# Delta rule on one Trainium2 core: the 16-to-32 step of the triangular inverse, from DVE products to matmuls

## The chip, the cores and the metric

The kernel runs on one core of one Trainium2 chip. The metric is the device time of one execution in microseconds; three timed runs of the kernel before gave 1537.31, 1538.44 and 1539.12, with a median of 1538.44 us.

## The reference

One decoder layer over 1024 tokens of width 1024, in float32. The normalised input is projected once; its columns feed four gated DeltaNet heads (head size 128) and eight forgetting-attention heads. Both outputs go through an output projection, a SwiGLU feed-forward block, a gated input embedding and a last norm. What the change touches is the triangular solve inside the chunked delta rule, cut here to its core:

```python
gc = jnp.cumsum(g, axis=-1)                    # per chunk of 64 tokens
kk = jnp.einsum('bnhid,bnhjd->bnhij', kb, k) * decay
a_mat = jnp.where(strict, kk, 0.0) + jnp.eye(CHUNK)
rhs = jnp.concatenate([vb, kb * jnp.exp(gc)[..., None]], axis=-1)
sol = lax.linalg.triangular_solve(a_mat, rhs, left_side=True, lower=True, unit_diagonal=True)
u, w = sol[..., :dv], sol[..., dv:]
...
v_new = u_c - jnp.einsum('bhcd,bhde->bhce', w_c, state)    # then a scan over the chunks
```

## The kernel before

All of the layer runs on one core, in stages: norm and value projection, then the stage of the change (from about 80 to 480 us of the span), then attention and output projection, then the feed-forward block and the rest.

In the stage of the change TensorE (PE) is fed from one order that is written out while the program is built. `weave` (line 221) holds a list of generators (the streams of the delta rule) and one filler, `projections` (line 670), whose `project` issues 24 matmuls `pj` of 512 columns for each half of a projected block. When a stream says it is ready, its matmuls are issued next; otherwise the filler gives one group of three. "Ready" is decided by `Plan` (lines 53 to 129), which keeps a clock of its own: a DVE operation on n elements is priced at 0.06 + n/960 us, an ACT operation at 0.09 + n/1200, a handoff from one engine to another at 0.377, one behind another on the same engine at 0.13, a DMA at 0.7 + bytes/360e3 + 1, and an f32 matmul of 128 columns at 4 x 128/2400. The order on PE is thus fixed: a matmul whose operand comes later than the plan thought stops PE, with the filler behind it.

The delta rule works in units of 128 tokens, eight for each head, handled as two groups g of four (tiles of 128 x 4 x 128). For each head h the streams are:

- `prep` (704): transposes, norms and gates; it makes nT (the negated strictly triangular matrix, transposed) and stores it to DRAM (n_d).
- `base` (765): all 32 blocks of 32 rows of the head's eight units, one partition for each (four copies over the 128 partitions), are read back as nb. DVE inverts 8-row blocks by seven steps, joins pairs to 16 rows (two products for each of the two 16-row blocks), and joins those to 32 rows (copies to uq, then four products: x times nb, then that times ub). A product is one `tensor_tensor` of 512 elements and one `tensor_reduce`. The blocks go to DRAM (u_d) by one DMA for the lower 16-row block and four for uq. `fence` makes later DVE work wait behind each of the three bursts.
- `inv` (824), twice for each head: loads U from u_d, transposes it on DVE in 32 x 32 blocks into T, then PE makes px = nT by T, ACT copies it, PE makes pz, and DVE writes pz into U where `mask` says so: the step from 32 to 64. A similar step on half the partitions goes from 64 to 128, and pw and pu follow.
- `scan` (901): the recurrence over eight units, whose pr, pS and po matmuls each wait for a small DVE operation (vT or Ss).

`prep_heads` and `inv_heads` order the heads: `prep` of head h+1 starts when `base` of head h is planned, `base` of head h+1 when `inv` of head h and `prep` of head h+1 are. Outside PE a scheduler orders each engine by the program; DVE, ACT and the SP queue, which issues nearly all DMAs, run in order. `gates` (513) makes ngc, the negated cumulative gate, which `prep` reads as a bias.

Of the kernel before, what the change touches and what calls it, by code (L numbers as in the profile page):

```python
# [8 lines left out]
F32 = mybir.dt.float32  # L9
# [3 lines left out]
I8 = mybir.dt.int8  # L13
AF = mybir.ActivationFunctionType
ALU = mybir.AluOpType
# [4 lines left out]
P = 128  # L20
S = 1024
DM = 1024
NT = S // P
KT = DM // P
HALF = 512
GH = 4
# [161 lines left out]
def hybrid_layer(ctx, tc, x, p, attn_norm_w, w_in, conv_w, a_log, dt_bias, gdn_norm_w, fox_f_bias,  # L188
# [3 lines left out]
    V, A, G, PE, SY = (Engine(tc, e, n) for e, n in zip((nc.vector, nc.scalar, nc.gpsimd, nc.tensor, nc.sync), "VAGPD"))  # L192
# [17 lines left out]
    def mm(ps, lhsT, rhs, start=True, stop=True, more=False):  # L210
        PE.matmul(ps, lhsT=lhsT, rhs=rhs, start=start, stop=stop, **(dict(skip_group_check=True) if more else {}))
# [31 lines left out]
    def ready(*ins, slots=(), extra=0.0):  # L243
        return poll(lambda: wait(*ins, slots=slots), extra)
# [21 lines left out]
    const = Pool(tc, name="const", bufs=1, side="left")  # L266
# [41 lines left out]
    B2 = HS // 4  # L308

    def dview(tl, offset, dims):  # L310
        a = tl[:]
        return bass.AP(tensor=a.tensor, offset=a.offset + offset, ap=dims)
# [77 lines left out]
    def gpt(name, tag="a"):  # L390
        return dict(a=psa, s=pss, o=pso)[tag].tile([P, 4, P], F32, tag=tag, name=name)
# [75 lines left out]
    mask = const.tile([P, P], I8, name="mask")  # L467
    V.scalar_tensor_tensor(mask, xm, 64.0, ge, op0=ALU.is_lt, op1=ALU.mult)

    xin.close()  # L470

    def load_w(c, name):
# [17 lines left out]
    def g4(tag, name, bufs=1, dt=F32, pool=None):  # L490
        pool = pool or (gpb if tag in ("scr", "nT", "X") else gp)
        return pool.tile([P, 4, P], dt, tag=tag, name=f"{tag}_{name}", bufs=bufs)
# [14 lines left out]
    egl = const.tile([P, NT, GH], F32, name="egl")  # L507
    egt = const.tile([P, NT, GH], F32, name="egt")
    kdw = const.tile([P, NT, GH], F32, name="kdw")
    ngc = const.tile([P, NT, GH], F32, name="ngc")  # L510
    beta = const.tile([P, NT, GH], F32, name="beta")

    def gates():
        def flat(tl):
            return tl.rearrange("p a b -> p (a b)")

        s0, s1, s2 = (flat(g4("scr", f"gates{i}", 4)) for i in range(3))
        zg, eg, ug, lgu = (s0[:, P * i:P * i + P].rearrange("p (t c) -> p t c", c=16) for i in range(4))
        ru = s1[:, 0:P].rearrange("p (t c) -> p t c", c=16)
        lf = s1[:, P:P + 64].rearrange("p (t c) -> p t c", c=FH)  # L520
        V.tensor_tensor(zg[:, :, 0:12], gat[:, :, 0:12], gb.unsqueeze(1).to_broadcast([P, NT, 12]), op=ALU.add)
        V.tensor_copy(zg[:, :, 12:16], gat[:, :, 12:16])
        V.tensor_scalar(zg[:, :, 0:8], zg[:, :, 0:8], -1.0, None, op0=ALU.mult)
        V.scalar_tensor_tensor(eg, zg, -1.0, zg, op0=ALU.mult, op1=ALU.min)
        A.activation(eg, eg, AF.Exp)
        V.tensor_scalar(ug, eg, 1.0, None, op0=ALU.add)
        A.activation(lgu, ug, AF.Ln)
        V.reciprocal(ru, ug)
        V.scalar_tensor_tensor(ug, ug, -1.0, eg, op0=ALU.add, op1=ALU.subtract)
        V.tensor_tensor(ug, ug, ru, op=ALU.mult)  # L530
        V.tensor_tensor(lgu, lgu, ug, op=ALU.subtract)
        V.scalar_tensor_tensor(lgu, zg, 0.0, lgu, op0=ALU.max, op1=ALU.add)
        V.scalar_tensor_tensor(beta, zg[:, :, 12:16], 0.0, eg[:, :, 12:16], op0=ALU.is_ge, op1=ALU.max)
        V.tensor_tensor(beta, beta, ru[:, :, 12:16], op=ALU.mult)
        V.tensor_scalar(lf, lgu[:, :, 0:8], -1.0, None, op0=ALU.mult)
        A.activation(alog, alog, AF.Exp)
        V.scalar_tensor_tensor(gg, lgu[:, :, 8:12], -1.0, alog.unsqueeze(1).to_broadcast([P, NT, GH]),
                               op0=ALU.mult, op1=ALU.mult)
        zz = gpa.tile([P, S], F32, tag="vt", name="zz", bufs=2)
        G.memset(zz, 0.0)  # L540
        yield from ready(gg)
        ggf, gcf, eglf, kdwf = (a.rearrange("p t h -> p (t h)") for a in (gg, gc, egl, kdw))
        gl = flat(gpt("gl"))
        mm(gl[:, 0:32], tri, ggf)
        mm(gl[:, 32:64], ones, ggf)
        V.tensor_copy(gcf, gl[:, 0:32])
        V.tensor_scalar(ngc.rearrange("p t h -> p (t h)"), gl[:, 0:32], -1.0, None, op0=ALU.mult)
        V.tensor_tensor(kdwf, gl[:, 32:64], gcf, op=ALU.subtract)
        A.activation(eglf, gl[:, 32:64], AF.Exp)
        A.activation(kdwf, kdwf, AF.Exp)  # L550
        A.activation(egt.rearrange("p t h -> p (t h)"), gcf, AF.Exp)
        crow = gpa.tile([P, S], F32, tag="vt", name="crow", bufs=2)[0:FH]
        G.memset(s2[0:FH], 1.0)
        for hf in range(2):
            ps = flat(gpt(f"lfT{hf}"))
            for j in range(4):
                tr(ps[0:FH, j * P:(j + 1) * P], lf[:, hf * 4 + j, :], ident)
            V.tensor_tensor_scan(crow[:, hf * HALF:(hf + 1) * HALF], s2[0:FH], ps[0:FH, :],
                                 0.0 if hf == 0 else crow[:, HALF - 1:HALF], op0=ALU.mult, op1=ALU.add)
        yield from ready(gc, slots=[SA])  # L560
        ps = flat(gpt("gcT"))
        tr(ps[0:32, 0:P], gcf, ident)
        gcs = s1[0:32, 2 * P:3 * P]
        A.activation(gcs, ps[0:32, 0:P], AF.Copy)
        SY.dma_start(gc_d, gcs)
        for img_ in u_d:
            SY.dma_start(img_.rearrange("(p a c) -> p a c", a=2, c=HS // 32),
                         zz[:, 0:HS // 32].unsqueeze(1).to_broadcast([P, 2, HS // 32]))
        cs_ = []
        for i in range(2):  # L570
            q = gpa.tile([P, 2, S], F32R, tag="kq", name=f"crs{i}", bufs=2)
            cs_ += [q[0:FH, 0], q[0:FH, 1]]
        split(cs_[0], cs_[1], crow)
        V.tensor_scalar(cs_[2], f(cs_[0]), -1.0, None, op0=ALU.mult)
        V.tensor_scalar(cs_[3], f(cs_[1]), -1.0, None, op0=ALU.mult)
        for a in range(4):
            SY.dma_start(crow_d[:, a, a // 2, :], f(cs_[a]))
            SY.dma_start(crow_d[:, a, 1 - a // 2, :].rearrange("h (b c) -> h b c", c=P),
                         ones[0:FH].unsqueeze(1).to_broadcast([FH, NT, P]))
        flags["gates"] = True  # L580
# [123 lines left out]
    def prep(h, g):  # L704
        kq, vT = kqv[h]
        nm = f"{h}_{g}"
        t0 = 4 * g
# [30 lines left out]
        V.tensor_tensor(dt_, egb, mbias.unsqueeze(1).to_broadcast([P, 4, P]), op=ALU.add)  # L738
        A.activation(egb, egb, AF.Exp)
        for j in range(4):  # L740
            A.activation(dt_[:, j, :], dt_[:, j, :], AF.Exp, bias=ngc[:, t0 + j, h:h + 1])
        yield from ready(sm, dt_, slots=[SA])
        nT = nTs[h, g] = g4("nT", nm, 4)
        qkT = qkTs[h, g] = g4("qkT", nm, 2 * home(h)[1], pool=home(h)[0])
# [20 lines left out]
    def base(h):  # L765
# [8 lines left out]
        pf = blk("pr")  # L774
        uf = blk("uq")
        u8 = uf[:, 192:448].rearrange("p (b r c) -> p b r c", b=4, c=8)
        uq = uf[:, 0:192].rearrange("p (m i n) -> p m i n", i=3, n=16)
        G.memset(ub, 0.0)
        G.memset(u8, 0.0)
        G.memset(u8.rearrange("p b r c -> p b (r c)")[:, :, 0:64:9], 1.0)  # L780
# [1 line left out]
        def sub(o, n):  # L782
            return nbt[:, o:o + 32 * n].rearrange("p (r c) -> p r c", c=32)[:, :, 0:n]

        def product(out, x, y):
            m, n = x.shape[1], x.shape[2]
            pr = pf[:, 0:m * n * n].rearrange("p (m n k) -> p m n k", n=n, k=n)
            V.tensor_tensor(pr, x.unsqueeze(2).to_broadcast([P, m, n, n]),
                            y.rearrange("p k n -> p n k").unsqueeze(1).to_broadcast([P, m, n, n]), op=ALU.mult)
            return V.tensor_reduce(out, pr, axis=AX.X, op=ALU.add)  # L790

        def fence(last, tile_):
            plan.fence = (last.ins.name, plan.done[plan.key(tile_)][0])
# [15 lines left out]
            last = product(ub[:, b, 0:8, 8:16], w, u8[:, 2 * b + 1])  # L809
        fence(last, ub)  # L810
        yield from ready(ub)
        for q in range(4):
            ps_ = slice(32 * q, 32 * q + 32)
            V.tensor_copy(uq[ps_, :, 0], ub[ps_, 0, 4 * q:4 * q + 4, :])
        for i, o, rhs in ((0, 2, sub(16, 16)), (2, 1, ub[:, 1])):
            for m in (0, 2):
                last = product(uq[:, m:m + 2, o], uq[:, m:m + 2, i], rhs)
        fence(last, uf)
        SY.dma_start(dview(u_d[h], B2 // 2, [[B2, 32], [P, 16], [1, 16]]), ub[0:32, 1])
        for q in range(4):  # L820
            SY.dma_start(dview(u_d[h], 4 * q * P, [[B2, 32], [P, 4], [1, 32]]),
                         uq[32 * q:32 * q + 32, :, 0:2].rearrange("p m i n -> p m (i n)"))

    def inv(h, g):
        nm = f"{h}_{g}"
# [7 lines left out]
        T = g4("X", f"T{nm}", 4)  # L833
        V.transpose(T.rearrange("p a b -> p (a b)"), U.rearrange("p a b -> p (a b)"))
        yield from ready(T, nT, slots=[SA])
        px = gpt(f"px5_{nm}")
        for j in range(4):
            mm(px[:, j, :], nT[:, j, :], T[:, j, :])
        X = g4("X", f"X{nm}", 4)
        A.activation(X, px, AF.Copy)  # L840
        yield from ready(X, slots=[SA])
        pz = gpt(f"pz5_{nm}")
# [926 lines left out]
```

## Time and profile before

| | |
|---|---|
| timed runs, median (lowest, highest) | 1538.44 us (1537.31, 1539.12) |
| the profiled execution's own time | 1536.84 us |
| its span, first to last instruction | 1535.1 us |
| PE busy, share of the span | 1444.3 us, 94% |
| DVE busy | 942.4 us, 61% |
| ACT busy | 628.5 us, 41% |
| mean granted TensorE clock | 0.98 |

The profiled execution is 1.6 us below the median. Matmuls overlap, so a PE that counts as busy need not be at its peak; where PE's queue stands still, the views give the wait and what ended it. The granted clock is in shares of 2.4 GHz; 0.50 is the level of 1.2 GHz.

### The profile page before, as it was taken

Reading aid. Unit: us, or ns where it says so; the run is one execution under the profiler, and the core shown is the slowest. Engines: PE = TensorE matmul, PEld = TensorE weight load, DVE = VectorE, ACT = ScalarE, POOL = GpSimd, SP = SyncE. Lnnn points to the kernel's source line nnn. Section 1 sums busy time; section 2 is a strip of 40 time slices with the busy share of each in tenths; the row PEclk is TensorE's granted clock in tenths of the full one; section 3 lists DMA queues with packets and bytes.
Section 4 is the critical chain, followed back from the end, with each engine's and each line's share of the span. In section 5 each row is a group of like instructions: output and inputs, shape, how many; then the busy total and the mean of one; then the engine's idle time right before and its main releaser. Section 6 shows DMA issues by size and latency. Waiting matters only on the chain.

```text
span 1535.1 us, 20340 instructions
## 1 busy us (share of the span) xinstructions
PE 1444.3 (94%) x7258; PEld 1205.0 (78%) x7258; DVE 942.4 (61%) x1966; ACT 628.5 (41%) x1395; POOL 383.0 (25%) x344
## 2 busy tenths in 40 slices
PE   7999898989898889999679999999999999999997
PEld 6988777777777768888558888888888788888886
DVE  6568879786533367757965555555555543426655
ACT  5345546454344577754523333333333321214322
POOL 3023222113242365663332222222221000000000
PEclk9999999999999899999889999999999999999999
DMA  7333322334347776746112222222224932312032
GB/s 214 117 91 71 85 62 86 96 86 138 119 137 209 231 209 157 174 150 188 49 55 83 83 83 82 83 83 82 83 83 134 336 99 87 112 43 83 28 104 89
DMA packets 189701, 175.93 MB, mean 115 GB/s; under 512 B 30864, under 2 KB 147136, under 8 KB 189600
## 3 DMA queue, kind: packets, MB, share of 16 engines
q1 hardware_dynamic: 189200, 174.06, 38.7%
q8 instruction: 57, 0.93, 0.3%
q0 software_dynamic: 400, 0.57, 0.2%
q14 instruction: 44, 0.36, 0.1%
HBM read 122.53 MB, written 52.07 MB: 114 GB/s over the span
## 4 chain that ended last, share of the span: by engine, by line
PE 63%; DVE 17%; DMA 8%; ACT 5%; issue 3%; SPq 1%; POOL 1%; ACTq 0%; DVEq 0%; POOLq 0%
PE dn L154 15%; PE gC L154 7%; PE gA L154 7%; PE gD L154 7%; PE ppg L154 6%; PE pj L154 4%; PE gB L154 4%; DVE scr_pr L154 3%; DVE y_g L154 3%; PE v L154 2%; DMA woraw<-in_w_out_dram 2%; DVE scr_uq L154 2%; PE wof L154 2%; SPq L154 1%; ACT p L154 1%
## 5 line engine op out<-in xcount | busy, mean ns | idle before, releaser
L154 PE MATMUL dn<-dn,ah 128*128 128x512 f32 x640 | 197.8, 390 | 1.6 <-DVE dn L154 1.6
L154 PE MATMUL pj<-xna,wh_u 128*128 128x512 f32 x384 | 162.2, 422 | 2.5 <-DVE pT L154 2.2
L154 PE MATMUL pj<-xna,wl_u 128*128 128x512 f32 x384 | 152.7, 398 | 0.0
L154 PE MATMUL pj<-xnb,wh_u 128*128 128x512 f32 x384 | 152.5, 397 | 0.0
L154 ACT ACTIVATE whP<-fraw 128x512 fp32r<-128x512 f32 x110 | 68.5, 629 | 193.0 <-issue 82.4
L154 PEld LDWEIGHTS dn<-dn,ah 128*128 128x128 f32 x640 | 119.9, 188 | 27.0 <-DVE dn L154 2.4
L154 PE MATMUL dn<-dn,al 128*128 128x512 f32 x320 | 124.5, 389 | 0.0
L154 POOL TENSOR_TENSOR wl_u<-wr_u,wh_u 128x512 fp32r<-128x512 f32 x48 | 70.2, 1483 | 172.5 <-ACT wh_u L154 137.4
L154 PE MATMUL gA<-hb_B,whP 128*128 128x512 f32 x352 | 110.1, 394 | 2.6 <-ACT p L154 2.6
L154 DVE TENSOR_TENSOR hr<-hr,dn 128x512 f32<-128x512 f32 x64 | 43.6, 684 | 109.8 <-PE dn L154 109.3
L154 PE MATMUL gD<-hb_T,whP 128*128 128x512 f32 x352 | 108.3, 389 | 0.0
L154 POOL TENSOR_TENSOR s<-fraw 128x512 f32<-128x512 f32 x22 | 28.8, 1311 | 284.6 <-DMA fraw<-in_w_gate_up_dram 281.0
L154 DVE TENSOR_TENSOR wlP<-s,whP 128x512 fp32r<-128x512 f32 x44 | 51.1, 1166 | 78.2 <-ACT whP L154 78.2
L154 DVE TENSOR_TENSOR wlP<-fraw,whP 128x512 fp32r<-128x512 f32 x110 | 78.6, 719 | 27.6 <-ACT whP L154 27.6
L154 POOL TENSOR_TENSOR p<-p,rc 128x384 f32<-128x384 f32 (+3 forms) x64 | 72.6, 1146 | 66.2 <-DVE rc L154 49.6
L154 PEld LDWEIGHTS pj<-xna,wh_u 128*128 128x128 f32 x384 | 74.0, 193 | 16.2 <-issue 2.4
L154 PEld LDWEIGHTS pj<-xna,wl_u 128*128 128x128 f32 x384 | 73.6, 192 | 16.6
L154 PEld LDWEIGHTS pj<-xnb,wh_u 128*128 128x128 f32 x384 | 74.2, 193 | 12.3
L154 ACT ACTIVATE ah<-ar 128x768 fp32r<-128x768 f32 (+1 forms) x32 | 25.3, 792 | 138.9 <-PE dn L154 133.8
L154 PEld LDWEIGHTS gA<-hb_B,whP 128*128 128x128 f32 x352 | 66.9, 191 | 16.9 <-ACT p L154 3.0
L154 PEld LDWEIGHTS gD<-hb_T,whP 128*128 128x128 f32 x352 | 66.1, 188 | 13.7
L154 PEld LDWEIGHTS dn<-dn,al 128*128 128x128 f32 x320 | 60.1, 188 | 12.5
(331 smaller groups left out, 3560.5 us busy)
## 6 DMA issues: line engine op xcount, KB each, us to landing
fraw<-in_w_gate_up_dram SPq DMA_DIRECT2D x44, 512.0 KB, 4.5
wr_u<-in_w_in_dram SPq DMA_DIRECT2D x24, 512.0 KB, 4.0
hb<-qk_d SPq DMA_DIRECT2D x24, 512.0 KB, 9.3
act_d<-th SPq DMA_DIRECT2D x44, 256.0 KB, 4.7
draw<-in_w_down_dram SPq DMA_DIRECT2D x22, 512.0 KB, 5.9
ar<-act_d SPq DMA_DIRECT2D x24, 384.0 KB, 3.7
v_d<-vs SPq DMA_DIRECT2D x16, 256.0 KB, 3.9
qk_d<-fsh SPq DMA_DIRECT2D x16, 256.0 KB, 2.4
```

The source lines that it names most:

```text
L154: r = f(*a, **kw)
```

## The change

`base` ends at blocks of 16 rows: the copies to uq, the four products and the third fence go, and two DMAs store the two 16-row blocks. `inv` gets one more step, from 16 to 32, in the form of the step from 32 to 64: px4 = nT by T, a copy by ACT, pz4, a masked copy into U with a new mask16, and a second transpose of U into T. The mask is built once at the start. Its room is found by writing the negated gate over gg, in place of ngc.

```diff
+    ge2 = xin.tile([P, P], F32, tag="ge2", name="ge2", bufs=1)
+    V.tensor_scalar(ge2, xm, 16.0, None, op0=ALU.is_ge)
+    mask16 = const.tile([P, P], I8, name="mask16")
+    V.scalar_tensor_tensor(mask16, xm, 32.0, ge2, op0=ALU.is_lt, op1=ALU.mult)
...
-    ngc = const.tile([P, NT, GH], F32, name="ngc")
...
-        V.tensor_scalar(ngc.rearrange("p t h -> p (t h)"), gl[:, 0:32], -1.0, None, op0=ALU.mult)
+        V.tensor_scalar(ggf, gl[:, 0:32], -1.0, None, op0=ALU.mult)
...
-        for q in range(4):
-            ps_ = slice(32 * q, 32 * q + 32)
-            V.tensor_copy(uq[ps_, :, 0], ub[ps_, 0, 4 * q:4 * q + 4, :])
-        for i, o, rhs in ((0, 2, sub(16, 16)), (2, 1, ub[:, 1])):
-            for m in (0, 2):
-                last = product(uq[:, m:m + 2, o], uq[:, m:m + 2, i], rhs)
-        fence(last, uf)
-        SY.dma_start(dview(u_d[h], B2 // 2, [[B2, 32], [P, 16], [1, 16]]), ub[0:32, 1])
-        for q in range(4):
-            SY.dma_start(dview(u_d[h], 4 * q * P, [[B2, 32], [P, 4], [1, 32]]),
-                         uq[32 * q:32 * q + 32, :, 0:2].rearrange("p m i n -> p m (i n)"))
+        for i in range(2):
+            SY.dma_start(dview(u_d[h], i * (B2 // 2), [[B2, 32], [P, 16], [1, 16]]), ub[0:32, i])
...
         yield from ready(T, nT, slots=[SA])
+        px = gpt(f"px4_{nm}")
+        for j in range(4):
+            mm(px[:, j, :], nT[:, j, :], T[:, j, :])
+        X = g4("X", f"Y{nm}", 4)
+        A.activation(X, px, AF.Copy)
+        yield from ready(X, slots=[SA])
+        pz = gpt(f"pz4_{nm}")
+        for j in range(4):
+            mm(pz[:, j, :], X[:, j, :], U[:, j, :])
+        V.copy_predicated(U, mask16.unsqueeze(1).to_broadcast([P, 4, P]), pz)
+        V.transpose(T.rearrange("p a b -> p (a b)"), U.rearrange("p a b -> p (a b)"))
+        yield from ready(T, slots=[SA])
         px = gpt(f"px5_{nm}")
```

## Rows read from the trace of the kernel before

**Rows 1.** Windows: us, busy (instructions) by engine, granted clock, DMA share, GB/s.

```profile
80.00:480.00 400.00, 373.49 (x1986) 310.05 (x1985) 284.67 (x687) 197.52 (x581) 105.37 (x93) 0.97 0.36 99
```

**Rows 2.** Waits of PE from 80 to 480: us in total, times, longest.

```profile
PE pS_s L154 <- DVE vT L154: 11.3, 9, 3.1
PE px L154 <- DVE ssq L154: 5.5, 1, 5.5
PE pr_s L154 <- DVE Ss L154: 5.5, 4, 2.5
PE pj L154 <- DVE pT L154: 2.2, 1, 2.2
PE pz L154 <- ACT X_X L154: 1.9, 2, 1.7
```

**Rows 3.** Timeline of PE, end of the stage: start, us, operation.

```profile
469.83 0.39 PE L154 MATMUL po_s<-Ss,kq 128*128 128x128 f32 x2
...
479.86 0.39 PE L154 MATMUL pj<-xna,wl_u 128*128 128x512 f32 x1
```

**Rows 4.** Timeline of PE at the long waits (in brackets: idle before, releaser).

```profile
181.83 1.41 PE L154 MATMUL px<-X_T,nT 128*128 128x128 f32 x5 [5.54 <-DVE ssq L154]
...
249.73 0.49 PE L154 MATMUL pr_s<-Ss,kq 128*128 128x128 f32 x2 [2.52 <-DVE Ss L154]
...
328.07 0.49 PE L154 MATMUL pS_s<-vT,ktok 128*128 128x128 f32 x2 [2.51 <-DVE vT L154]
...
407.38 0.79 PE L154 MATMUL pS_s<-vT,ktok 128*128 128x128 f32 x2 [2.08 <-DVE vT L154]
```

**Rows 5.** Windows around three of these waits (columns as in rows 1).

```profile
180.00:200.00 20.00, 17.92 (x92) 14.68 (x93) 15.96 (x51) 16.67 (x56) 3.63 (x3) 0.86 0.32 85
240.00:260.00 20.00, 17.11 (x90) 14.20 (x89) 16.99 (x55) 12.18 (x54) 2.67 (x2) 0.91 0.40 117
...
400.00:420.00 20.00, 17.92 (x102) 15.58 (x100) 5.75 (x13) 10.05 (x30) 5.02 (x4) 0.91 0.50 161
```

**Rows 6.** Groups of DVE by form, 140 to 420: busy us, mean ns | idle before.

```profile
L154 DVE TENSOR_TENSOR scr_pr<-scr_uq,nb 128x512 f32<-128x512 f32 x16 | 18.1, 1134 | 0.2
L154 DVE TENSOR_REDUCE scr_uq<-scr_pr 128x32 f32<-128x512 f32 x16 | 11.0, 685 | 0.2
...
L154 DVE TENSOR_TENSOR scr_pr<-scr_uq,scr_ub 128x512 f32<-128x512 f32 x8 | 9.6, 1197 | 0.1
...
L154 DVE COPY_PREDICATED U<-mask,pz 128x512 f32<-128x512 int8 x8 | 5.8, 733 | 5.4 <-PE pz L154 5.4
L154 DVE STREAM_TRANSPOSE X_T<-U 128x512 f32<-128x512 f32 x8 | 5.7, 710 | 8.6 <-DMA U<-u_d 8.3
...
L154 DVE COPY scr_uq<-scr_ub 32x64 f32<-32x64 f32 x16 | 3.8, 236 | 0.2
```

**Rows 7.** Timeline of DVE, third burst of head 0 and what follows.

```profile
166.19 0.78 DVE L154 COPY scr_uq<-scr_ub 32x64 f32<-32x64 f32 x4
...
174.24 0.69 DVE L154 TENSOR_REDUCE scr_uq<-scr_pr 128x32 f32<-128x512 f32 x1
...
180.97 0.71 DVE L154 STREAM_TRANSPOSE X_T<-U 128x512 f32<-128x512 f32 x1 [1.14 <-DMA U<-u_d]
```

**Rows 8.** Timeline of the SP queue, head 0's stores and loads of u_d.

```profile
174.95 1.74 SPq L154 DMA_DIRECT2D u_d<-scr_uq  x4
...
177.94 0.93 SPq L154 DMA_DIRECT2D U<-u_d  x2
```

**Rows 9.** Timeline of PE: four matmuls px of one group, and the next.

```profile
260.26 1.06 PE L154 MATMUL px<-X_T,nT 128*128 128x128 f32 x8
261.15 0.39 PE L154 MATMUL pS_s<-vT,ktok 128*128 128x128 f32 x2
```

**Rows 10.** Groups of ACT by form, 140 to 440 (columns as in rows 6).

```profile
L154 ACT ACTIVATE X_X<-px 128x512 f32<-128x512 f32 x8 | 4.6, 582 | 0.4 <-PE px L154 0.3
```

**Rows 11.** The mask, built once: duration in ns, start in us.

```profile
L154 DVE SCALAR_TENSOR_TENSOR mask<-xm,ge x1: 282/282/282, 20.4 to 20.4; 128x128 int8<-128x128 f32 x1
```

More of the change, by code (lines that the diff above doesn't have):

```diff
@@ L740, in prep @@
         for j in range(4):
-            A.activation(dt_[:, j, :], dt_[:, j, :], AF.Exp, bias=ngc[:, t0 + j, h:h + 1])
+            A.activation(dt_[:, j, :], dt_[:, j, :], AF.Exp, bias=gg[:, t0 + j, h:h + 1])
         yield from ready(sm, dt_, slots=[SA])
@@ L776, in base @@
         u8 = uf[:, 192:448].rearrange("p (b r c) -> p b r c", b=4, c=8)
-        uq = uf[:, 0:192].rearrange("p (m i n) -> p m i n", i=3, n=16)
         G.memset(ub, 0.0)
@@ L838, in inv @@
             mm(px[:, j, :], nT[:, j, :], T[:, j, :])
-        X = g4("X", f"X{nm}", 4)
         A.activation(X, px, AF.Copy)
```

## The prediction

> **What bounds the kernel now.** I first read busy time by stage in the windows. From 80 to 480 us, where the delta rule runs, PE is busy 373.5 of 400 us, at a mean granted clock of 0.97 [rows 1]. The view of PE's waits then explains the rest: its five rows sum to 26.4 us, of which 22.3 stand behind vT, Ss or the first px, that is behind DVE [rows 2]. The reader should see that no row names a shortage of work: the filler pj never runs dry. At the stage's end the last matmul of the scan starts at 469.83, and pj go on until 479.86 plus 0.23, about 480.1 [rows 3]. So the heads' chain has about 10 us to spare, and what sets the end of the stage is PE's sum: its work, its stops and its slow stretches. The stages behind it start when the pj are done, so I carry a shift of this end through to the end of the kernel.
>
> The timeline of PE shows where the stops are. Head 0's px starts after 5.54 us; one scan matmul stops PE for 2.52 us during head 1's `base`, one for 2.51 us during head 2's, and one for 2.08 us while head 3's U is on its way [rows 4]. The windows give a second price: around such a stop the granted clock is 0.86 or 0.91 [rows 5]. In 20 us, 0.91 is 0.09 x 20 = 1.8 us lost; the stretch is at 1.2 GHz after PE stood still for 2.52 or 2.08 us. For 0.86 it is 2.8 us, but part of that lies inside the stop itself, and I count 1.8 there too.
>
> Why PE stops follows from the plan. A product is priced as two operations of 0.593 us with 0.13 behind each, 1.45 us; the rows have 1.134 or 1.197 and 0.685 us, 1.82 to 1.88 [rows 6]. The order on PE counts on an earlier DVE than there is, and PE pays the difference.
>
> **The change part by part.** *Removed on DVE.* Per head two products with nb, two with ub, and four copies: 2 x 1.134 + 2 x 1.197 + 4 x 0.685 + 4 x 0.236 = 8.3 us, 33 us over four heads [rows 6]. Head 0's burst runs from 166.19 to 174.24 + 0.69 = 174.93, with one foreign operation of 0.6 in it [rows 7], which agrees. DVE is busy 284.7 of 400 us [rows 1], so this time as such is worth nothing. What counts is its lateness against the plan: four products at 5.8 and the copies at 0.64 are 6.4 us in the plan, so about 2 us per head, and two scan stops of 2.5 us stand right behind this burst [rows 4].
>
> *Stores.* Four DMAs of uq took 1.74 us to issue, and T starts 6.0 us after the burst's end [rows 7, 8]. Two issues at the same rate (0.44 each) take 0.9 us, so U comes about 0.9 us closer behind its burst.
>
> *Stops that go.* Head 0: 2.2 of the 5.54 (lateness) plus 0.9 (stores), 3.1. Heads 1 and 2: 2.52 + 2.51 = 5.0. Head 3: about 0.9 of 2.08, since its stop is behind U, not the burst. Sum 9.1 us. The bounds are 0 (something else is late in their place) and 22.3 (all stops behind DVE) [rows 2].
>
> *Slow stretches that go.* Those behind the stops of heads 1 and 2 go, and I take half of the other two: 3 x 1.8 = 5.4 us. Bounds: 0, and all of it, (1 - 0.97) x 400 = 12 us [rows 1].
>
> *Added on PE.* Sixteen groups of four matmuls of 128 columns. From the start of one such group to the next instruction is 261.15 - 260.26 = 0.89 us [rows 9]; 16 x 0.89 = 14.2 us. They come when U and X are there, not while PE stands still, so nothing hides them: filler displaced by them has to run later.
>
> The Trainium skill, TensorE: Matmul & The Clock Gate, section Back-to-back issue gap, gives about 81 ns a matmul at 128 columns in a sustained stream (its examples are bf16). Estimated from that figure, 64 matmuls would cost 5.2 us and the sum below would be 9 us lower. The trace disagrees: 0.89 us for four is 0.22 us each, of the very form that is added, in f32 and two records for each [rows 9].
>
> *Added handoffs.* Each of the eight `inv` gets an ACT copy (0.582) [rows 10], a masked copy (0.733) and a transpose (0.710) [rows 6], against 0.517, 0.593 and 0.593 in the plan: 0.32 us late in each. The step of the same form cost PE 1.9 us in eight groups [rows 2]. 8 x 0.32 = 2.6 if all of it shows, 1.9 by that row; I take 2.5. Bounds: 0, and 8 times the longest wait for X, 8 x 1.7 = 13.6. Queued behind the new masked copy and transpose on DVE stand the other group's work, `prep`'s and the scan's vT and Ss, for which PE's next pr or pS waits.
>
> *Latency of a head.* `base` becomes 8.3 + 0.9 = 9.2 us shorter. The new step takes 0.89 + 0.58 + 0.89 + 0.73 + 0.71 = 3.8 us of work, for two groups on the same engines up to 7.6, and four handoffs at 0.4. It is even within some 2 us a head, 8 us over four, inside the 10 us of spare [rows 3].
>
> *Setup.* The second mask is two operations like that of 0.28 us at 20.4 us [rows 11]; DVE's slack covers them, and without it they would cost 0.6 us. Writing the negated gate over gg is the same operation in another place, after the matmuls that read gg, whose result it needs anyway: 0.
>
> *Sum.* 14.2 - 9.1 - 5.4 + 2.5 = +2.2 us. The profiled execution took 1536.84, so 1539.0; it lies 1.6 below the median, so against the median 1538.44 + 2.2 = 1540.6 us.
>
> **The rivals.** *Slower: the waits only move.* In place: DVE's in-order queue. A scan's vT or Ss ends up behind a masked copy that waits for pz4 or a transpose that waits for U, as head 3's vT does now [rows 4]. If the stops stay at about today's sum, only some 3 of the 9.1 and 2 of the 5.4 us come back: 14.2 - 3 - 2 + 2.5 = +11.7, 1550.1. It decides once the four heads together keep over 18 of the 22.3 us. For it: the plan's prices are unchanged, two bursts are left that are as late as the one that goes, and the new step adds operations that the plan prices too low. Against it: the stops named in rows 4 do stand behind the burst that goes.
>
> *Faster: the third burst was most of the lateness.* Lateness adds up from burst to burst, and the last one lets it show. If the stops behind DVE fall by 16 of 22.3 us and four slow stretches go (7.2), with 1.5 for handoffs: 14.2 - 16 - 7.2 + 1.5 = -7.5, 1530.9. For it: head 0's 5.54 us shows as one stop at the end. Against it: heads 1 to 3 have stops in the first two bursts as well; the nine waits for vT sum to 11.3 us and the longest is 3.1 [rows 2].
>
> *The chain becomes the bound.* If a head grows by over 2.5 us, four use up the 10 us of spare, and the scan's tail stands without filler: at 4.5 us a head, 18 - 10 = 8 more than the sum, +10, 1548.6. For it: both groups share ACT and DVE with `prep` of the next head. Against it: `base` gives 9.2 us back on the same chain, and `prep` starts earlier too.
>
> **How the numbers follow.** Within 0.2%, about 3.1 us, a measurement of this kernel can't be told from no change. The forecast, with its own range of -3 to +7 us, has 0.38: 0.28 of it is the same, 0.08 slower, 0.02 faster. The moved waits have 0.30, all slower. The fuller gain has 0.24, all faster. The chain has 0.08, 0.05 slower and 0.03 the same. That makes 0.26 faster, 0.31 same, 0.43 slower. The range runs from 1531, the middle of the faster case, to 1551, just over the middle of the moved waits; what is left out is the outer half of each, under 2 in 10.
>
> **What the profile would show.** Right: 16 more px and pz groups of about 0.89 us; no copies to uq, and 16 fewer products; the first px of head 0 after a stop of 2 to 3 us instead of 5.54; no stop of 2 us or more behind the end of `base` in heads 1 and 2; a clock over 0.97 from 80 to 480; the last pj at about 482. Wrong: waits of PE for vT, Ss and px still over 18 us in sum, or under 7; a gap without pj after the last scan's matmuls; or a shift behind the stage, in attention's start, of more than 2 us that the stage's end doesn't have.

## The result, and the profile after

| | median, us | lowest to highest | runs |
|---|---|---|---|
| before | 1537.88 | 1535.44 to 1539.12 | 4 |
| after | 1550.07 | 1548.36 to 1551.74 | 4 |

The changed kernel is slower: ratio 1.0081 [1.0062, 1.0099], about 12.2 us where 2.2 had been forecast. Its profiled execution took 1550.98 us with a span of 1549.3, which is 14.2 us of span more than before.

First the windows of the changed kernel: the delta-rule stage, the three stretches of [rows 5], and the stretch from the last projection to the first output product `wof`.

```profile
80.00:480.00 400.00, 379.64 (x2098) 319.42 (x2096) 261.24 (x653) 200.27 (x585) 99.88 (x92) 0.98 0.35 95
180.00:200.00 20.00, 17.36 (x87) 15.03 (x86) 16.24 (x46) 11.33 (x29) 4.86 (x7) 0.78 0.18 51
240.00:260.00 20.00, 16.15 (x99) 14.52 (x98) 11.13 (x49) 12.93 (x58) 0.55 (x1) 0.91 0.39 118
400.00:420.00 20.00, 19.01 (x96) 15.84 (x97) 12.46 (x24) 7.93 (x24) 10.13 (x7) 1.00 0.64 200
485.00:702.00 217.00, 189.21 (x1157) 160.10 (x1156) 126.08 (x273) 134.70 (x323) 117.38 (x117) 0.94 0.68 184
```

Against [rows 1] DVE does 23 us less from 80 to 480, and PE is busy 6.1 us more and idle 6.1 us less. The clock around 400 us is full now, around 250 it is what it was, and around 190 it is lower than before (0.78, where [rows 5] have 0.86).

The end of the stage, in PE's timeline:

```profile
474.77 0.39 PE L154 MATMUL po_s<-Ss,kq 128*128 128x128 f32 x2
...
484.81 0.39 PE L154 MATMUL pj<-xna,wl_u 128*128 128x512 f32 x1
```

Both ends are about 4.95 us later than in [rows 3], with the same 10 us between them. So 5.0 us of the 14.2 arise in the stage. Behind it, the first `wof` starts at 688.29 before and at 702.20 after: from the last pj that is 208.4 and 217.4 us, another 9.0. From the first `wof` to the end of the span it is 846.8 and 847.1, no difference.

PE's waits from 80 to 480, after (us in total, times, longest):

```profile
PE pr_s L154 <- DVE Ss L154: 7.3, 5, 3.8
PE pz L154 <- ACT X_Y L154: 3.6, 2, 2.6
PE px L154 <- ACT scr_sq L154: 3.4, 1, 3.4
PE pj L154 <- DVE pT L154: 3.3, 2, 2.2
PE px L154 <- DVE qkT L154: 1.1, 1, 1.1
PE px L154 <- DVE X_T L154: 0.7, 1, 0.7
```

With two rows of half a microsecond or less they sum to 20.3, where [rows 2] sum to 26.4. The 11.3 us behind vT are gone. New are waits behind ACT: for `X_Y`, the copy of the new step, and for `scr_sq`, which is the next head's preparation. PE's timeline places them in head 0:

```profile
166.00 0.60 PE L154 MATMUL tk<-ident,kq 128*128 128x128 f32 x4
...
172.07 1.13 PE L154 MATMUL px<-X_T,nT 128*128 128x128 f32 x8 [0.68 <-DVE X_T L154]
...
178.64 2.07 PE L154 MATMUL px<-X_T,nT 128*128 128x128 f32 x8 [3.35 <-ACT scr_sq L154]
...
183.36 2.08 PE L154 MATMUL pz<-U,X_Y 128*128 128x128 f32 x8 [2.64 <-ACT X_Y L154]
...
245.62 0.49 PE L154 MATMUL pr_s<-Ss,kq 128*128 128x128 f32 x2 [3.85 <-DVE Ss L154]
```

The one stop of 5.54 us in [rows 4] has become three, 6.67 us in sum. In whole heads, all stops counted, the timelines give 5.8, 5.3, 7.7 and 5.5 us before for heads 0 to 3, and 6.7, 5.4, 2.2 and 2.7 after: heads 2 and 3 give back 8.3 us, heads 0 and 1 take 1. ACT's timeline shows what head 0's PE waited for:

```profile
176.45 0.63 ACT L154 ACTIVATE xb_g<-y_g 128x512 f32<-128x512 f32 x1 [7.15 <-DVE ssq L154]
176.98 0.58 ACT L154 ACTIVATE ktok<-tk 128x512 f32<-128x512 f32 x1
...
179.21 0.33 ACT L154 ACTIVATE scr_sq<-tk 128x128 f32<-128x128 f32 x1
...
181.49 1.33 ACT L154 ACTIVATE scr_dt<-scr_dt,gg 128x128 f32<-128x128 f32 x4
182.66 0.65 ACT L154 ACTIVATE X_Y<-px 128x512 f32<-128x512 f32 x1
...
184.27 1.32 ACT L154 ACTIVATE scr_dt<-scr_dt,gg 128x128 f32<-128x128 f32 x4
185.43 0.64 ACT L154 ACTIVATE X_Y<-px 128x512 f32<-128x512 f32 x1
```

The first px ends near 173 and its copy X_Y starts at 182.66. ACT works its queue in order, and in front of X_Y stands `prep` of head 1: copies of tk, sums of squares, exponentials. They in turn stand behind an `xb_g` that waits 7.15 us for DVE. DVE is late for the reason that its own timeline shows:

```profile
171.21 0.71 DVE L154 STREAM_TRANSPOSE X_T<-U 128x512 f32<-128x512 f32 x1 [3.42 <-DMA U<-u_d]
173.43 0.71 DVE L154 STREAM_TRANSPOSE X_T<-U 128x512 f32<-128x512 f32 x1 [1.51 <-DMA U<-u_d]
174.07 2.28 DVE L154 SCALAR_TENSOR_TENSOR y_g<-xb_g,cw,y_g 128x512 f32<-128x512 f32 x3
```

The transposes wait for U's DMA, and the convolution's y_g stand in order behind them. The second group's px waits in PE because the preparation still holds one of the three PSUM buffers of `psa`: the releaser is scr_sq, which reads tk there.

Head 1's stop of 3.85 us has a queue behind it too, and here it is DVE's. The small operation Ss, for which PE waits, stands in order behind a transpose that waits for U's DMA:

```profile
243.76 0.71 DVE L154 STREAM_TRANSPOSE X_T<-U 128x512 f32<-128x512 f32 x1 [2.67 <-DMA U<-u_d]
...
245.26 0.30 DVE L154 SCALAR_TENSOR_TENSOR Ss<-Ss,egl,pS_s 128x128 f32<-128x128 f32 x1
```

In attention the waits of PE with the largest sums were, from 480 to 688 before:

```profile
PE pp L154 <- ACT pst L154: 4.7, 1, 4.7
PE lg L154 <- ACT p L154: 4.5, 4, 2.7
PE pT L154 <- DVE ptl L154: 3.2, 6, 1.0
```

and from 485 to 702 after:

```profile
PE lg L154 <- ACT p L154: 9.5, 3, 7.6
PE pT L154 <- ACT pst L154: 7.6, 2, 7.1
PE pT L154 <- DVE ptl L154: 5.3, 5, 3.9
```

The 7.6 us for `p` have a plain chain behind them, on PE and then on ACT:

```profile
577.64 0.80 PE L154 MATMUL lg<-hb 128*128 128x256 f32 x2 [7.62 <-ACT p L154]
```

```profile
575.70 0.63 ACT L154 ACTIVATE wog<-woraw 128x512 fp32r<-128x512 f32 x1 [6.35 <-DMA woraw<-in_w_out_dram]
576.23 0.58 ACT L154 ACTIVATE pth<-pT 128x512 fp32r<-128x512 f32 x1
576.71 0.79 ACT L154 ACTIVATE p<-lg,mx 128x640 f32<-128x640 f32 x1
```

A conversion of the output weights, `wog<-woraw`, waits in ACT's queue for its load, and attention's exponentials stand behind it. The loads are late: the first goes out at 518.64 before and here at

```profile
553.92 0.97 SPq L154 DMA_DIRECT2D woraw<-in_w_out_dram  x2
```

They are issued once all eight units of the input-embedding products pp (two halves each) are done. The written order of the kernel before does most of these in a gap ahead of attention's third block of transposes (pT0_4), and the last starts at 515.96. In the changed kernel that planned gap has closed, the products are spread over attention's first 18 score blocks, and the last starts at 551.35. None of the diff's lines touches them; the planner's clock alone moved them.

### The profile page after: what moved, and what is told of

It is laid out like the page before. It is cut to its first block, busy times and chain, and to the rows that moved or that the text cites. A ratio compares the mean times of both kernels' runs of the same rounds, so it can differ in the third digit from the quotient of the medians.

```text
span 1549.3 us, 20567 instructions
## 1 busy us (share of the span) xinstructions
PE 1455.2 (94%) x7386; PEld 1218.1 (79%) x7386; DVE 922.7 (60%) x1936; ACT 631.5 (41%) x1403; POOL 378.3 (24%) x344
## 4 chain that ended last, share of the span: by engine, by line
PE 59%; DVE 5%; DMA 3%; ACT 3%; issue 2%; POOL 1%; SPq 0%; ACTq 0%; POOLq 0%; DVEq 0%
PE dn L154 15%; PE gC L154 7%; PE gA L154 7%; PE gD L154 7%; PE ppg L154 6%; PE gB L154 4%; PE wog L154 2%; PE po L154 2%; PE pj L154 2%; PE wof L154 2%; PE lg L154 2%; PE pT L154 1%; DMA woraw<-in_w_out_dram 1%; DMA pp_d<-pst 1%; PE tp_n L154 1%
## 5 line engine op out<-in xcount | busy, mean ns | idle before, releaser
L154 POOL TENSOR_TENSOR wl_u<-wr_u,wh_u 128x512 fp32r<-128x512 f32 x48 | 66.3, 1402 | 201.8 <-ACT wh_u L154 166.0
L154 PEld LDWEIGHTS gD<-hb_T,whP 128*128 128x128 f32 x352 | 66.1, 188 | 13.7
```

Source lines behind the costliest of these rows:

```text
L154: r = f(*a, **kw)
```

## The experiments

Twelve kernels ran, in three sets with before beside them, whose median was 1536.6 to 1536.7 in each. Ratios are to that; differences in us below are of medians. "Held" means one more condition in `fox2`, which does all pp ahead of attention's third block:

```
-            while n1[0] <= n or n3[0] < n // 2 - 1:
+            while n1[0] <= n or n3[0] < n // 2 - 1 or (n == 2 and n_ple[0] < NT):
```

In the kernel before all pp stand ahead of that block already, and the program is the same with this condition and without it; so its times serve for "before, held" too.

| kernel | median, us | ratio, interval |
|---|---|---|
| after, held | 1546.55 | 1.0051 [1.0031, 1.0070] |
| before, pp spread | 1540.28 | 1.0016 [1.0005, 1.0028] |
| before, pp spread later | 1554.61 | 1.0122 [1.0107, 1.0137] |
| both steps, held | 1552.04 | 1.0090 [1.0071, 1.0108] |
| neither step, held | 1532.98 | 0.9977 [0.9960, 0.9993] |
| before, prices corrected, held | 1547.39 | 1.0077 [1.0065, 1.0089] |
| after, prices corrected, held | 1532.35 | 0.9975 [0.9962, 0.9988] |
| before, head 1 prepared at 7.5, held | 1538.50 | 1.0007 [0.9992, 1.0022] |
| after, head 1 prepared at 7.5, held | 1529.93 | 0.9956 [0.9943, 0.9969] |
| before, head 1 prepared at 12, held | 1550.37 | 1.0088 [1.0073, 1.0102] |
| after, head 1 prepared at 12, held | 1528.39 | 0.9950 [0.9937, 0.9963] |
| after, head 1 prepared at 12, not held | 1523.67 | 0.9903 [0.9882, 0.9923] |

**Attention's part.** The changed kernel, held.

> The changed kernel, with the third block of attention's transposes held until all sixteen input-embedding products pp have been issued, which is where they stand in the kernel before. Theory (the matmuls cost about 5 us in the delta-rule stage, and the other 9 us of the profile come from pp and the output-projection loads standing later in the order): the end of the pj stays at 485, the stretch from there to the first wof falls from 217 to about 209, and the time is 1543 (1540 to 1546). Rival (attention is slower because the stage before it ends later and its loads meet others, whatever the order of pp): 1549 to 1551.

In the profile attention's stretch is 208.2 us again, as before; the stage's end, 485.77, is 1.0 us later. The median, 1546.55, lies a little over the range given and below the rival's. The span fell by 7.3 us, the median by 3.5. So the order of pp and loads is a cause; its size in timed runs is nearer 4 than 9 us, and 9.9 us over the kernel before are left with the order of pp restored. The six runs lie between 1541.44 and 1548.68, and the profiled one took 1543.71: one pair of profiles doesn't settle a few microseconds.

The same from the other side: before, with each pp unit allowed only from a given score block on.

```
-            if ple_ready():
+            if n1[0] >= (0, 2, 4, 6, 7, 10, 15, 18)[n_ple[0]] and ple_ready():
```

> The kernel before, with pp spread over attention's first 18 score blocks, about as in the changed kernel; the delta rule untouched. Theory of the order: the end of the pj stays at 480, and the time is 1545 to 1549, 7 to 11 us over the kernel before, with long waits of PE while the output-projection weights load. Rival (the order of pp matters little, the later end of the delta rule does it): 1536 to 1540.

It came out at the rival's upper end, 1540.28; attention's stretch is 212.3, so 3.9 longer, but the last pj is 1.9 earlier in that profile, though PE's order up to it is that of the kernel before. As the theory had the mechanism and missed the size, the blocks were moved on to (0, 3, 6, 9, 12, 15, 18, 21):

> The kernel before with the eight input-embedding products spread later still over attention's score blocks, to the 21st, so that the loads of the output weights start 47 planned us later than in the kernel before and not 29 as in the first spread kernel. Theory (the later the products and the loads behind them, the longer attention): the stretch from the last projection to the first output product, 208.4 us in the kernel before and 212.3 in the first spread kernel, is 215 to 219 us and the time is 1542 to 1547. Rival (attention takes the loads wherever they come, and what the changed kernel lost there has another cause): 211 to 213 us and 1538 to 1541.

It was more than either: 1554.61, and 222.7 us for the stretch. Here again ACT's conversion waits for its load and PE for p behind it:

```profile
586.24 0.80 PE L154 MATMUL lg<-hb 128*128 128x256 f32 x2 [6.53 <-ACT p L154]
```

```profile
584.30 0.63 ACT L154 ACTIVATE wog<-woraw 128x512 fp32r<-128x512 f32 x1 [5.42 <-DMA woraw<-in_w_out_dram]
```

An order that no line of the change touches is thus worth up to 18 us in the unchanged kernel.

**The two halves of the change.** Both steps: the changed kernel, with the third burst on DVE and its stores kept, and the second mask all zero, so that the matmul step runs and changes nothing.

```
-    V.scalar_tensor_tensor(mask16, xm, 32.0, ge2, op0=ALU.is_lt, op1=ALU.mult)
+    V.scalar_tensor_tensor(mask16, xm, 0.0, ge2, op0=ALU.is_lt, op1=ALU.mult)
...
+        for i, o, rhs in ((0, 2, sub(16, 16)), (2, 1, ub[:, 1])):
+            for m in (0, 2):
+                last = product(uq[:, m:m + 2, o], uq[:, m:m + 2, i], rhs)
...
```

> Both ways to 32 rows: DVE's third burst stays and the four stores of uq with it, and the matmul step is added with a mask of zeros, so that it copies nothing and U stays as DVE made it; pp held as in the first run. Theory (the matmuls are paid in full on PE and the removed burst gives part of it back): the delta-rule stage is 14 to 19 us longer than before, 1552 to 1557. Rival (the added matmuls mostly fill time in which PE stood still): under 1546.

Neither step: the burst gone and px4, its copy, pz4, the masked copy and the second transpose gone too.

```
-        px = gpt(f"px4_{nm}")
...
-        V.transpose(T.rearrange("p a b -> p (a b)"), U.rearrange("p a b -> p (a b)"))
-        yield from ready(T, slots=[SA])
```

> Neither way: DVE ends at 16 rows and the matmul step is left out, so the step from 16 to 32 rows is not computed; pp held as in the first run. Theory (the third burst costs PE about 9 us in stops and slow stretches, of which the changed kernel gets most back): 1527 to 1532. Rival (the burst costs PE nothing, since DVE is busy only 71% of the stage, and the stops move elsewhere): 1536 to 1540.

With the burst in place the matmul step costs 1552.04 - 1536.7 = 15.3 us, without it 1546.55 - 1532.98 = 13.6; the forecast had 14.2 for its matmuls, 16.7 with its handoffs. Removing the burst alone returns 3.7 us, 1 us short of the theory's range and 3 from the rival's; with the matmul step there it returns 1552.04 - 1546.55 = 5.5. Both are far from the forecast's 14.5 (9.1 + 5.4). The waits of PE in the kernel with neither step say where the rest stayed:

```profile
PE pS_s L154 <- DVE vT L154: 8.6, 5, 4.3
PE pr_s L154 <- DVE Ss L154: 6.7, 4, 2.9
PE pz L154 <- ACT X_Y L154: 3.6, 1, 3.6
PE px L154 <- ACT scr_sq L154: 3.0, 1, 3.0
```

The collision of head 0 stands here too, 3.6 and 3.0 us, without a matmul of the new step. With both steps it is not there: the first px has the stop of the kernel before, and the waits for `X_Y` in head 0 are 0.36 and 0.48 us.

```profile
182.56 2.04 PE L154 MATMUL px<-X_T,nT 128*128 128x128 f32 x8 [5.48 <-DVE ssq L154]
```

So the collision comes from taking the burst away: `inv` of head 0 starts some 10 us sooner, and lands on the preparation of head 1.

**Head 0's collision.** In the changed kernel, held, `prep` of head 1 starts 12 planned us after the base of head 0 instead of 3 (`L_C`).

```
-            yield L_C
+            yield 12.0 if h == 1 else L_C
```

> The changed kernel with the eight input-embedding products kept ahead of attention's third block of transposes, and the preparation of head 1 started 12 instead of 3 planned us after the base blocks of head 0 are issued. Theory (in head 0 the return was lost because the copies of the matmul step stand on ACT, and its PSUM buffer is held, behind work of head 1's preparation): head 0's stops of PE, 6.67 us in the changed kernel, fall to 3 us or less, the delta-rule stage ends at 480 to 483 instead of 484.8 to 485.8, and the time is 1541 to 1545 against 1546.6 with the products held alone. Rival (what head 0 gains, head 1 gives back, because its own preparation is then late): the stage ends at 484 to 487 and the time is 1545 to 1549.

1528.39: 18.2 us less than the same kernel without it, over three times the gain expected, and 8 less than before. PE's timeline shows the preparation's transposes tk behind the first group's step and no longer ahead of it:

```profile
171.58 1.13 PE L154 MATMUL px<-X_T,nT 128*128 128x128 f32 x8 [0.94 <-DVE X_T L154]
177.51 2.08 PE L154 MATMUL pz<-U,X_Y 128*128 128x128 f32 x8 [2.71 <-ACT X_Y L154]
180.66 1.19 PE L154 MATMUL px<-X_T,nT 128*128 128x128 f32 x8
181.69 0.60 PE L154 MATMUL tk<-ident,kq 128*128 128x128 f32 x4
```

Head 0's stops are 3.65 us, not below 3 but half of 7.3. The larger part came later: the sum of all stops to 485 us is 13.9, where it was 20.7, and the last pj is at 473.72.

That a later start is simply better was the obvious rival, so the same edit went into the kernel before:

> The kernel before with the preparation of head 1 started 12 instead of 3 planned us after the base blocks of head 0 are issued, the same edit that took the changed kernel from 1546.6 to 1528.4. Theory (the edit helps the changed kernel because its matmul step met head 1's preparation on ACT and in PSUM; the kernel before has no such step in head 0): the kernel before gains little, 1533 to 1540, and changed against before is then worth some 5 to 10 us with both prepared late. Rival (the late preparation is simply a better order for either kernel, and the change itself still costs 8 to 12 us): 1517 to 1523.

It made it slower by 13.7, outside both ranges and on the other side of no change. Its timeline shows the same collision, moved:

```profile
174.31 1.47 PE L154 MATMUL tk<-ident,kq 128*128 128x128 f32 x12
...
186.13 3.78 PE L154 MATMUL px<-X_T,nT 128*128 128x128 f32 x16 [6.90 <-ACT scr_sq L154]
```

With the burst in place, `inv` of head 0 starts near 181 us [rows 4]. A preparation at 3 does its tk from 165.40 to 172.8; ACT still reads them until 183.3, but the first px goes at 181.83, as soon as its T is there. One at 12 meets it: T is there at 181.9, and px starts at 186.13. Without the burst `inv` starts at 172, and it is the preparation at 3 that meets it. Between them, at 7.5:

> The kernel before with the preparation of head 1 started 7.5 planned us after the base blocks of head 0. With before_prep_late it shows how far the kernel before moves by this order alone. Theory: within 5 us of 1536.6, so 1532 to 1541, because its stop behind the base (5.5 us in head 0) is DVE's burst itself, which no start of the preparation shortens. Rival (better order for either kernel): below 1528.

> The changed kernel, with the input-embedding products held ahead of attention's third block, and the preparation of head 1 started 7.5 planned us after the base blocks of head 0. Theory (what counts is that the preparation's reads of PSUM and its exponentials come behind the copies of the matmul step on ACT): the third stop of head 0, pz waiting for the copy of px, is still there, and the time lies between those at 3 and at 12 us: 1531 to 1542. Rival (any other order of the planner's gives another time by chance): above 1545 or below 1526.

1538.50 is no change, as the theory had it, but not for its reason: head 0's stop, 5.07 us, is now a tk that waits for ACT's scr_sq. 1529.93 lies 1 us below its range, with the wait of pz for X_Y still there at 3.31 us. The last run of this kind drops the hold:

> The changed kernel with the late preparation of head 1 alone (12 planned us), and the input-embedding products not held. In its planned order these products fall back into a gap ahead of attention's third block by themselves, at nearly the planned times of the kernel before. Theory (late preparation is enough): 1526 to 1532, the stretch from the last projection to the first output product 203 to 207 us. Rival (attention still loses its 9 us without the hold): 1535 to 1541.

1523.67, faster than the range given, with a stretch of 197.7 us. Its profiled execution is the fastest of its six, 1514.50, over 9 us below their median, so the profile shows its best case. There PE has a granted clock of 1.00 from 80 to 480:

```profile
80.00:480.00 400.00, 384.77 (x2156) 1.00 0.38 105
```

This is the fastest version seen: the change, with one number of the planner moved. The kernel before ran at 3, 7.5 and 12 and with other prices, and was fastest as it is, at 1536.6 to 1536.7; between the best of each there are 13 us.

**The planner's prices.** The prices of DVE's broadcast products were set to n/480 and of their sums to n/850, in place of n/960.

```
-            dur = {"V": 0.06 + n / 960,
+            v = 0.06 + n / (480 if name == "tensor_tensor" and "scr_pr" in self.key(outs[0]) else 850 if name == "tensor_reduce" else 960)
+            dur = {"V": v,
```

> The kernel before, with only the planner's prices on DVE changed: 0.06 us + n/480 for the broadcast products of the base blocks and n/850 for their sums, in place of n/960 for both, and the eight input-embedding products kept ahead of attention's third block of transposes. Theory (PE stops behind each head's base blocks because the planner takes DVE's products for half as long as they are): the stops of PE behind the bases of heads 0 to 3 fall from 23 us to under 8, the projections end at 465 to 475 instead of 479.9, and the time is 1526 to 1535. Rival (the planner then finds no work to put in the longer wait, and the scan of the last head is left without cover): the stops only change their place, the time is 1537 to 1546.

> The changed kernel with the same corrected prices on DVE and the input-embedding products kept ahead of attention's third block of transposes. Theory (the changed kernel's 20 us of stops are the planner's too low prices): the stage ends at 476 to 481 and the time is 1538 to 1543. Rival (its stops are ACT's and the in-order queue's, which these prices don't touch): the stage ends at 484 to 487 and the time is 1545 to 1550.

The rival held for the kernel before, 1547.39: the stops only moved (12.5 us of PE's pj now wait for ACT's xb_g, 9.4 for vT), and the last scan runs to 510 us, behind the last pj at 475.91. For the changed kernel the theory's direction held and its size was too small: 1532.35, a gain of 14.2 where 3.5 to 8.5 were expected. Head 0 still stops there, for 5.53 us in a tk that waits for ACT's scr_sq; so a gain of this size doesn't need head 0's collision to go.

## Why the prediction was off

To compare kernels whose ends lie apart, I take PE from 80 us to the first `wof`. The windows of that stretch, for before, after, after at 12 (held) and before at 12 (columns: us, PE busy, granted clock, DMA share, GB/s):

```profile
80.00:688.29 608.29, 563.01 (x3142) 0.97 0.47 129
```

```profile
80.00:702.20 622.20, 574.05 (x3276) 0.97 0.47 128
```

```profile
80.00:677.62 597.62, 567.61 (x3274) 0.99 0.48 131
```

```profile
80.00:699.24 619.24, 567.74 (x3140) 0.96 0.46 126
```

Idle is the length less the busy time. What the clock cost is summed over windows of 1 us, busy time times what the granted clock lacks of full. The rest is work at full clock. Each row is one execution. How far one execution moves is seen in the kernel before with pp spread, where PE's order to the last pj is unchanged: there the clock cost 7.5 us from 80 to 480, where the kernel before has 10.3.

| kernel | length | work | idle | lost to the clock |
|---|---|---|---|---|
| before | 608.3 | 546.7 | 45.3 | 16.3 |
| after | 622.2 | 561.2 | 48.1 | 12.8 |
| after, held | 614.0 | 560.3 | 40.9 | 12.8 |
| both steps, held | 620.3 | 564.9 | 45.7 | 9.7 |
| neither step, held | 606.5 | 546.8 | 42.6 | 17.1 |
| before, at 12, held | 619.2 | 544.3 | 51.5 | 23.4 |
| after, at 12, held | 597.6 | 560.1 | 30.0 | 7.5 |

- *Added on PE*, 14.2: right within some 2 us, which is what this reading allows: kernels with the same matmuls have 546.7, 546.8 and 544.3. The work is 561.2 - 546.7 = 14.5 us more, 13.6 and 13.4 in the other two rows of the changed kernel, 13.5 from neither step to held, and 15.8 between the two at 12. Both steps, with 18.2, stand apart, which is not explained. The estimate from the Trainium skill, TensorE: Matmul & The Clock Gate, section Back-to-back issue gap, 5.2 us, is excluded by this row. The Trainium skill, FP8 and Floating Point Precision, section TensorE Precision Notes, gives four passes for true f32, which is in the direction of what the rows show: 0.22 us a matmul and not 0.08 [rows 9].
- *Stops that go* and *Added handoffs*, together -6.6: right in sum within the stage of this one pair of profiles, -6.1, and wrong in place. (The parts of the 9.1 add up to 9.0.) Head 0, of which 3.1 was expected back, lost 0.9; the line on a first px behind a stop of 2 to 3 us failed. Heads 2 and 3 gave more than was said, head 1 nothing: its stop of 3.85 us, behind the end of `base`, breaks the line on heads 1 and 2.
- *Slow stretches that go*, -5.4: mis-sized. By the same sum the clock cost 10.3 us from 80 to 480 before and 7.1 after, so 3.2 came back, hardly more than the 2.8 by which an unchanged order moves; the stretch around head 0 got slower. With 14.5 - 6.1 - 3.2 the stage comes to +5.2, and the profile has +5.0.
- The two terms of the burst together, 9.1 + 5.4 = 14.5, are where the timed runs differ most from the forecast: taking the burst away returned 3.7 us without the matmul step and 5.5 with it. From before to neither step the table has 2.7 us less idle time and 0.8 more lost to the clock. The matmul step with its handoffs, 16.7, cost 13.6 to 15.3.
- *"The stages behind it start when the pj are done, so I carry a shift of this end through to the end of the kernel"*: this step failed too. In the profiles it carried 5.0, and 9.0 more arose in attention, by the order of pp and loads; the timed runs put that order at 3.5. The text had named a shift in attention's start of more than 2 us as what would prove it wrong, and gave it no price. By medians the miss is thus 9.9 us instead of 2.2 with the order of pp restored, and 3.5 more without (13.4 against the kernel before of these sets, 12.2 against the one beside the first runs); how the 9.9 divide between the stage (5.7 in the profile up to the first `wof`) and the rest stays open.
- *Slower: the waits only move* had the median to the tenth, 1550.1, which is luck. Its own condition, over 18 of 22.3 us kept behind DVE, is not met: vT is gone, and what is left for Ss and px sums to 12.5, whoever releases it. Its place, DVE's queue behind a transpose that waits for U, is what stopped head 1 for 3.85 us; in head 0 the in-order queue was ACT's, behind work of `prep`, and attention's part was in none of its terms. In the kernel with neither step vT, Ss and px keep 18.3 us, 3.0 of them behind ACT: there the waits in the main did only move. *Latency of a head* and *the chain becomes the bound*: the spare is 10 us as before.
- That the range, which ended at 1551, held 1550.07 is luck as well: what made the time was in good part outside the terms that it was drawn from.

What lies under these failures is in the main one thing. All terms were worked out for a fixed order, but removing the burst moves the start of `inv` by some 10 us against a `prep` that is placed by a count from the base, and the planner's clock against attention's gap. That this is so in head 0 is shown; for the whole it is argued from how the change's worth swings when only the order is moved, and that any other order gives another time by chance isn't excluded: the kernel before too moves by 10.8 and 13.7 us with other prices and at 12. The change against the kernel before, in the same setting of that order, is worth +9.9 us at 3 (both held), -8.6 at 7.5, -22.0 at 12, and -15.0 with corrected prices. The added work is about 14 us each time; the rest returns between 4 and 36. Why later heads gain so much when head 0's collision is gone is seen in the sums (idle 40.9 to 30.0, clock 12.8 to 7.5) and was not taken apart further; nor was the difference of 4.7 us that the hold makes at 12.

## What to carry to other kernels

Price a change that shortens one stream under at least two placements of the streams around it: here the work was priced right within some 2 us, and the sign still hung on how the next head's preparation was placed. When the order on the engines is written by a planner, ask first which gap in its plan will close and what uses that gap, however far behind the edit it stands. And where an operation that waits for a DMA stands in an engine's in-order queue, look at what is queued behind it: here scan operations and attention's exponentials paid for that wait. The sign of it is idle time of that engine that ends with a DMA.

## What the runs showed of the hardware

PE's granted clock fell after single stops (around the one of 2.52 us in [rows 4] it is 0.91 over 20 us [rows 5]), but the sums of idle time and of what the clock cost did not always move together. In the kernel before at 12, 6.2 us more idle time goes with 7.1 us more lost to the clock; in the changed kernel at 12, 10.9 us less (against held) goes with 5.3 us less. Against that, the changed kernel has 2.8 us more idle time than the kernel before and 3.5 less lost to the clock. That the clock's loss follows from the stops was not tried by itself. A stretch of 400 us with a granted clock of 1.00 was reached with PE busy 384.8 of it. ACT, at 41% busy over the span of the kernel before, was the engine whose queue held PE up in head 0 and in attention; in head 1 it was DVE's, for 3.85 us.
